# Where the rows of the second half are staged before they are normalised, and one persistent buffer for raw weights

## The chip, the cores and the metric

One Trainium2 chip, of which the kernel uses one core. The metric is device time in microseconds for one call. The engines are TensorE (PE; its weight loads are shown as PEld), VectorE (DVE), ScalarE (ACT), GpSimd (POOL) and SyncE (SP), which here only issues transfers. Each takes its own instructions strictly in order; semaphores tie them together.

## What is computed

One layer of a hybrid decoder trunk for 2048 new prompt positions and 64 sample tokens, width 1024. Every row of x is RMS-normalised and multiplied by one input projection with 33 column groups of 128; 16 of them belong to a short convolution, 17 to an RWKV-7 recurrence of 8 heads.

```python
xn = rms_norm(x, norm_g)
p = xn @ w_in
pc, pr = p[..., :CONV_COLS], p[..., CONV_COLS:]
u = cg * h
z = conv_w[0]*u_ext[:, 0:T] + conv_w[1]*u_ext[:, 1:T+1] + conv_w[2]*u_ext[:, 2:T+2]
y_conv = bg * z * silu(gc)
# recurrence, per head and token:
S = S * w_t + sa * (kk_t * a_t) + v_t * k_t ;  o_t = S r_t
y = concat([y_conv, y_rwkv]) @ w_out
return x + y, ...            # then a final rms_norm
```

## The kernel before

The prompt is worked in two halves of 1024 positions. A half has three blocks of columns (positions): block 0 with 256 positions (in the first half also with the sample tokens), blocks 1 and 2 with 384 each. `xprep(hf)` prepares a half: for each block it loads the rows (128 positions x 1024) into staging buffers, takes the sum of squares of each on ACT (L247), computes the reciprocal root on DVE (`rsqrt`, a chain of small operations), scales each row and multiplies it by the norm's weights `grow`, which lie in la0 (L263 on DVE; the third row of blocks 1 and 2 by an ACT scaling and a POOL multiplication, L260 and L261), transposes the row on PE into two PSUM banks `ax` (L282) and splits each result into a rounded high part `xh` (ACT) and the remainder `xl` (DVE, L207). So a block of 128 positions costs eight transposes, two ACT copies and two DVE subtractions. The banks `ax` are two.

`project` multiplies: for each column group and block 24 matmuls into one of two PSUM banks `pj` (xh and xl against wh, and xh against wl, over 8 row groups), then an evaluation `evac` frees the bank. In the first half `load_w` loads the raw weights of a column group in two halves into `wr`, splits them into wh and wl (ACT and POOL) and also writes these to memory (`wsp`); in the second half it loads wh and wl from there, by transfers that POOL issues, and `wr` isn't used.

There are eight steps s, four head pairs in each half: `rwkv_pair` (projections of the pair), `inverse` (a small triangular inverse: on DVE a long substitution of operations sub and xi, whose result goes to memory and back, dx, and is combined by small products `cx` on PE), `wkv` (the recurrence, a chain between PE and DVE), and `conv_group`. At step 3 the order is `rwkv_pair`, `conv_group`, `xprep(1)`, `inverse`, `wkv`, so the second half's rows are prepared while conv group 3 and the inverse of pair 3 run.

The buffers in question: tag hp, four buffers of 128x1108, hold a pair's k and rr, a conv group's u and z, and staged rows. la0 and la1 hold the low-rank inputs of a half (la), which are free between the halves; la0 then takes `grow`. `wr` is a tag with two half tiles of 128x512; the output tiles (`out_tile`, the last stage) use the same tag for scratch that nobody reads. A block's xh and xl can be overwritten when the last projection of the first half, conv group 3's, is through with that block.

The code is recorded in program order; a scheduler then decides the order on each engine and of the transfers, with its own estimates of durations, and puts the semaphores. So a change of buffers changes the order.

Of the kernel before, what the change touches and what calls it, by code (L numbers as in the profile page):

```python
# [10 lines left out]
BF16 = mybir.dt.bfloat16  # L11
# [6 lines left out]
D = 1024  # L18
CW = 512
HD = 64  # L20
KT = D // 128
# [57 lines left out]
def half_blocks(hf):  # L79
    if hf == 0:  # L80
        return [Blk(0, 330, 74, 256, 0, True, SAMP), Blk(1, 384, 0, 384, 256, False, SAMP),
                Blk(2, 384, 0, 384, 640, False, SAMP)]
    return [Blk(0, 256, 0, 256, 0, False, 0), Blk(1, 384, 0, 384, 256, False, 0),
            Blk(2, 384, 0, 384, 640, False, 0)]
# [3 lines left out]
def trunk_kernel(ctx, tc, I, O):  # L88
# [8 lines left out]
    cnt = [0]  # L97

    def T(pool, shape, tag, bufs=1, dt=F32):
        cnt[0] += 1  # L100
        return pools[pool].tile(shape, dt, tag=tag, bufs=bufs, name=f"{tag}_{cnt[0]}")
# [42 lines left out]
    def rowtile():  # L144
        return T("half", [128, HALF + SAMP], "la0", 1)[:, :D]
# [5 lines left out]
    def load_params():  # L151
        act.dma_start(out=cst[:, 128:], in_=I["consts"][:, 128:])
        act.dma_start(out=prm, in_=I["params"])
        act.dma_start(out=stc, in_=I["state_conv"])
# [50 lines left out]
    def split(hi, lo, src, eng=dve):  # L205
        copy(hi, src)
        eng.tensor_tensor(out=lo, in0=src, in1=hi.bitcast(F32), op=ALU.subtract)  # L207

    def xprep(hf):
        grow = rowtile()  # L210
        if hf == 1:
            act.dma_start(out=grow, in_=I["norm_g"].partition_broadcast(128).rearrange("p a d -> p (a d)"))
        if hf == 0:
            act.dma_start(out=cst[:, 0:128], in_=I["consts"][:, 0:128])
        xh, xl = [], []
        stage = [0]

        def staging():
            stage[0] += 1
            if stage[0] % 6 == 5:  # L220
                return T("half", [128, HALF + SAMP], "la1", 1)[:, :D]
            if stage[0] % 6 == 0 and hf == 0:
                return T("pair", [128, 32, 32], "na", 1).rearrange("p a b -> p (a b)")
            return T("half", [128, 1108], "hp", 4)[:, :D]

        for bl in half_blocks(hf):
            h = T("xn", [128, KT, bl.cols], f"xh{bl.i}", 1, F32R)
            l = T("xn", [128, KT, bl.cols], f"xl{bl.i}", 1, F32R)
            xh.append(h)
            xl.append(l)  # L230
            rows = []
            if bl.samp:
                rows.append((I["x_sample"], SAMP, bl.c0 + 128))
            for i in range(bl.np // 128):
                tok = hf * HALF + bl.p0 + i * 128
                rows.append((I["x_prompt"][tok:tok + 128, :], 128, bl.c0 + i * 128))
            ss = T("small", [128, 3], "ssx", 2)[:, :len(rows)]
            if bl.samp:
                pool.memset(ss, 1.0)
            xts = []  # L240
            for j, (src, n, o) in enumerate(rows):
                xt = staging()[:n]
                sync.dma_start(out=xt, in_=src)
                junk = l[:n, :, o:o + 128]
                if hf == 1:
                    junk = T("ch", [128, KT, 128], "c2", 4, BF16)
                act.activation(out=junk, in_=xt.rearrange("p (k c) -> p k c", k=KT), func=AF.Square,  # L247
                               accum_out=ss[:n, j:j + 1])
                xts.append(xt)
            if bl.samp:  # L250
                sync.dma_start(out=grow, in_=I["norm_g"].partition_broadcast(128).rearrange("p a d -> p (a d)"))
                sr = T("small", [128, 144], "sub", 1)[:, :KT * NB].rearrange("p (k b) -> p k b", k=KT)
                act.dma_start(out=sr, in_=I["state_shift"])
                load_params()
            dve.tensor_scalar(out=ss, in0=ss, scalar1=1.0 / D, scalar2=RMS_EPS, op0=ALU.mult, op1=ALU.add)
            r = rsqrt(ss, len(rows), 128, "n")
            for j, xt in enumerate(xts):
                n = rows[j][1]
                if bl.i and j == 2:
                    copy(xt, xt, scale=r[:n, j:j + 1])  # L260
                    pool.tensor_tensor(out=xt, in0=xt, in1=grow[:n], op=ALU.mult)  # L261
                else:
                    stt(xt, xt, r[:n, j:j + 1], grow[:n])  # L263
            if bl.samp:
                pool.memset(h[:, :, 72:74].bitcast(F32), 0.0)
                pool.memset(l[:, :, 72:74].bitcast(F32), 0.0)
                hv = h[:, :, 0:72].rearrange("p k (b j) -> p k b j", j=9)
                lv = l[:, :, 0:72].rearrange("p k (b j) -> p k b j", j=9)
                split(hv[:, :, :, 0], lv[:, :, :, 0], sr)
                xt = xts.pop(0)  # L270
                rows.pop(0)
                pool.dma_start(out=O["shift_s"], in_=xt[7:SAMP:8, :])
                ps = AX([128, KT, SAMP])
                for k in range(KT):
                    pe.transpose(out=ps[:, k, :], in_=xt[:, k * 128:(k + 1) * 128], identity=ident[:SAMP, :SAMP])
                split(hv[:, :, :, 1:9], lv[:, :, :, 1:9], ps.rearrange("p k (b j) -> p k b j", j=8))
            for xt, (_, _, o) in zip(xts, rows):
                for q in range(2):
                    ps = AX([128, 4, 128])
                    for k in range(4):  # L280
                        kk = q * 4 + k
                        pe.transpose(out=ps[:, k, :], in_=xt[:, kk * 128:(kk + 1) * 128], identity=ident)  # L282
                    split(h[:, q * 4:q * 4 + 4, o:o + 128], l[:, q * 4:q * 4 + 4, o:o + 128], ps)
            if hf == 1 and bl.i == 2:
                act.dma_start(out=O["shift_p"], in_=xts[-1][127:128, :])
        return xh, xl
# [3 lines left out]
    def load_w(src, col=None, hf=0):  # L290
        wh = T("w", [128, KT, 128], "wh", 2, F32R)
        wl = T("w", [128, KT, 128], "wl", 2, F32R)
        if hf == 1:
            pool.dma_start(out=wh, in_=wsp[col, 0])  # L294
            pool.dma_start(out=wl, in_=wsp[col, 1])
            return wh, wl
        for q in range(2):
            wr = T("w", [128, 4, 128], "wr", 2)
            sync.dma_start(out=wr, in_=src[:, q * 4:q * 4 + 4, :])
            split(wh[:, q * 4:q * 4 + 4, :], wl[:, q * 4:q * 4 + 4, :], wr, pool)  # L300
        sync.dma_start(out=wsp[col, 0], in_=wh.bitcast(F32))
        sync.dma_start(out=wsp[col, 1], in_=wl.bitcast(F32))
        return wh, wl
# [589 lines left out]
    def out_tile(woh, wol, frow, ysrc, rows, xsrc, dst):  # L893
        yr = T("half", [128, HALF + SAMP], "la1", 1)[:, :D].rearrange("p (k t) -> p k t", k=KT)[:, :, :rows]
        sync.dma_start(out=yr, in_=ysrc.rearrange("(k p) t -> p k t", p=128))
        yh = T("w", [128, KT, 128], "wh", 2, F32R)[:, :, :rows]
        yl = T("w", [128, KT, 128], "wl", 2, F32R)[:, :, :rows]
        copy(yh, yr, scale=0.5)
        stt(yl, yr, 0.5, yh.bitcast(F32), ALU.mult, ALU.subtract)
        xt = T("half", [128, 1108], "hp", 4)[:, :D][:rows]  # L900
        sync.dma_start(out=xt, in_=xsrc)
        ss = T("small", [128, 2], "ss2", 2)[:rows]
        junk = T("w", [128, D], "wr", 2, BF16)[:rows]
        for q in range(2):
            ps = PS([128, 512], "pj", 2)[:rows]
            cs = slice(q * 512, (q + 1) * 512)
            for k in range(KT):
                mm(ps, yh[:, k, :], woh[k][:, cs], start=(k == 0), stop=False)
                mm(ps, yh[:, k, :], wol[k][:, cs], start=False, stop=False)
                mm(ps, yl[:, k, :], woh[k][:, cs], start=False, stop=(k == KT - 1))  # L910
            tt(xt[:, cs], ps, xt[:, cs], ALU.add)
            act.activation(out=junk[:, cs], in_=xt[:, cs], func=AF.Square, accum_out=ss[:, q:q + 1])
        s = T("small", [128, 1], "ss", 2)[:rows]
        tt(s, ss[:, 0:1], ss[:, 1:2], ALU.add)
        dve.tensor_scalar(out=s, in0=s, scalar1=1.0 / D, scalar2=RMS_EPS, op0=ALU.mult, op1=ALU.add)
        r = rsqrt(s, 1, rows)
        stt(xt, xt, r, frow[:rows])
        act.dma_start(out=dst, in_=xt)
# [7 lines left out]
    for s in range(8):  # L926
        hf, p = divmod(s, NPAIR)
# [95 lines left out]
```

## Time and profile before

| | us |
|---|---|
| three runs | 1623.73, 1629.85, 1634.08 (median 1629.85) |
| profiled execution, device time | 1627.34 |
| its span | 1625.4 |
| PE busy, PEld busy | 1517.5 (93%), 1267.9 (78%) |
| DVE, ACT, POOL busy | 1011.9 (62%), 616.3 (38%), 290.4 (18%) |
| mean granted clock of PE | 0.966 of 2.4 GHz |

Busy time counts from the start to the end of an instruction, pipelined neighbours together; where an engine waits, the trace names what ended the wait. A granted clock of 0.50 is 1.2 GHz, of 1.00 2.4 GHz. Issue of a transfer and its landing are apart by microseconds; the trace gives both.

### The profile page before, as it was taken

What the parts mean: (1) busy time and instruction counts of PE and PEld (TensorE: products, weight loads), DVE (VectorE), ACT (ScalarE), POOL (GpSimd) and SP (SyncE); (2) the same over time, 40 slices, a digit from 0 to 9 for tenths busy, and PEclk for the clock granted to TensorE, in tenths of its full rate; (3) what the DMA queues carried; (4) which work ended last, traced back from release to release, by engine and by line L of the source; (5) the groups of instructions that cost most, each with busy time, mean ns of one, the idle gap of its engine ahead of it and who ended that gap; (6) DMA issues with size and microseconds to landing.
All of it is one profiled execution on the core that took longest, in us unless ns stands there. A gap on an engine that the chain in (4) does not pass through costs nothing.

```text
span 1625.4 us, 29341 instructions
## 1 busy us (share of the span) xinstructions
PE 1517.5 (93%) x11088; PEld 1267.9 (78%) x11088; DVE 1011.9 (62%) x3101; ACT 616.3 (38%) x1591; POOL 290.4 (18%) x395
## 2 busy tenths in 40 slices
PE   4999999989999999879999899999998999899997
PEld 4988877877788778867789678977896788667885
DVE  7387458655687458775587258635863587466544
ACT  6452345324532354344451245134413533342221
POOL 3133103311133112320022002200220022000000
PEclk9999999899999998989999899999999999899999
DMA  7323412242043213341123212321241135414441
GB/s 239 117 83 126 122 44 96 84 121 81 19 131 112 94 49 113 124 137 60 36 62 109 67 35 63 108 68 36 61 124 53 36 100 158 144 61 136 141 138 52
DMA packets 121967, 151.90 MB, mean 93 GB/s; under 512 B 62617, under 2 KB 86681, under 8 KB 121826
## 3 DMA queue, kind: packets, MB, share of 16 engines
q1 hardware_dynamic: 107024, 104.53, 20.9%
q0 software_dynamic: 9536, 34.64, 6.7%
q10 hardware_dynamic: 5266, 10.86, 1.8%
q8 instruction: 88, 1.44, 0.4%
q14 instruction: 53, 0.43, 0.1%
HBM read 92.60 MB, written 57.35 MB: 92 GB/s over the span
## 4 chain that ended last, share of the span: by engine, by line
PE 63%; DVE 22%; DMA 6%; issue 5%; ACT 3%; SPq 1%; POOL 1%; ACTq 0%; DVEq 0%; POOLq 0%
PE pj L129 41%; PE ca L129 5%; PE ax L129 5%; DVE sub L123 5%; DVE xi L123 4%; PE cb L129 4%; PE oo L129 2%; DVE hp L123 2%; PE cx L129 2%; PE cx L699 1%; DMA hp<-in_x_prompt 1%; DMA dx<-xi 1%; DVE hp L120 1%; DMA AB<-dx 1%; DMA na<-dn 1%
## 5 line engine op out<-in xcount | busy, mean ns | idle before, releaser
L129 PE MATMUL pj<-xh,wh 128*128 128x384 f32 (+3 forms) x1856 | 654.8, 353 | 17.4 <-DVE hp L123 13.7
L129 PE MATMUL pj<-xl,wh 128*128 128x384 f32 (+3 forms) x1856 | 652.6, 352 | 2.6 <-POOL xl L207 1.9
L129 PE MATMUL pj<-xh,wl 128*128 128x384 f32 (+3 forms) x1856 | 652.0, 351 | 0.6 <-DMA wl<-wsp 0.6
L129 PEld LDWEIGHTS pj<-xh,wh 128*128 128x128 f32 x1856 | 356.3, 192 | 50.1 <-DVE hp L123 11.2
L129 PEld LDWEIGHTS pj<-xl,wh 128*128 128x128 f32 x1856 | 356.8, 192 | 31.4 <-POOL xl L207 2.8
L129 PEld LDWEIGHTS pj<-xh,wl 128*128 128x128 f32 x1856 | 355.4, 191 | 28.1 <-issue 2.0
L117 ACT ACTIVATE tS<-sv,wc 64x64 f32<-64x64 f32 x256 | 88.0, 344 | 118.7 <-DVE sv L120 95.6
L207 POOL TENSOR_TENSOR wl<-wr,wh 128x512 fp32r<-128x512 f32 x66 | 87.6, 1338 | 195.1 <-ACT wh L117 191.7
L120 DVE SCALAR_TENSOR_TENSOR sv<-cb,wc,tS 64x64 f32<-64x64 f32 x240 | 68.0, 283 | 62.7 <-PE cb L129 55.0
L129 PE MATMUL ax<-L,bk 64*128 64x128 f32 x528 | 79.4, 299 | 21.0 <-DVE bk L123 12.7
L129 PEld LDWEIGHTS ax<-L,bk 64*128 64x128 f32 x528 | 66.3, 198 | 38.0 <-issue 23.2
L123 DVE TENSOR_TENSOR sub<-xi,na 128x126 f32<-128x126 f32 (+22 forms) x248 | 79.8, 322 | 16.3 <-DMA na<-dn 9.2
L117 ACT ACTIVATE t<-pj,prm 128x384 f32<-128x384 f32 (+3 forms) x170 | 68.9, 433 | 53.5 <-PE pj L129 52.4
L747 DVE TENSOR_SCALAR u<-ca,Q 128x64 f32<-128x64 f32 x128 | 36.2, 283 | 81.2 <-PE ca L129 81.0
L527 POOL TENSOR_TENSOR bk<-t,t 64x384 f32<-64x384 f32 (+2 forms) x56 | 58.0, 1036 | 144.4 <-ACT t L499 78.3
L123 DVE TENSOR_TENSOR xi<-xi,sub 128x126 f32<-128x126 f32 (+22 forms) x248 | 76.8, 310 | 7.3
L117 ACT ACTIVATE wh<-wr 128x512 fp32r<-128x512 f32 x66 | 40.5, 625 | 94.6 <-PE pj L129 74.5
L129 PEld LDWEIGHTS ca<-sv,L 128*64 128x64 f32 x528 | 43.7, 134 | 38.1 <-DVE sv L120 13.8
L737 DVE COPY xs<-ca 128x64 f32<-128x64 f32 x128 | 28.7, 224 | 66.2 <-PE ca L129 57.0
L129 PE MATMUL ca<-sv,L 128*64 128x64 f32 x528 | 68.7, 245 | 0.1
L294 POOL DMA_DIRECT2D wh<-wsp x33 | 18.7, 567 | 273.9 <-PE pj L129 199.6
L123 DVE TENSOR_TENSOR hp<-pj,hp 128x512 f32<-128x512 f32 (+1 forms) x34 | 23.4, 689 | 62.7 <-PE pj L129 62.3
(203 smaller groups left out, 2064.7 us busy)
## 6 DMA issues: line engine op xcount, KB each, us to landing
wr<-in_w_in SPq DMA_DIRECT2D x66, 256.0 KB, 3.7
wsp<-wh SPq DMA_DIRECT2D x33, 512.0 KB, 2.9
wsp<-wl SPq DMA_DIRECT2D x33, 512.0 KB, 3.9
wh<-wsp POOLq DMA_DIRECT2D x33, 512.0 KB, 3.6
wl<-wsp POOLq DMA_DIRECT2D x33, 512.0 KB, 4.5
hp<-in_x_prompt SPq DMA_DIRECT2D x29, 512.0 KB, 4.0
la<-yd SPq DMA_DIRECT2D x16, 512.0 KB, 4.0
out_y_p<-hp ACTq DMA_DIRECT2D x16, 512.0 KB, 2.6
```

The source lines that it names most:

```text
L117: act.activation(out=out, in_=in_, func=AF.Copy, scale=scale, bias=bias)
L120: eng.scalar_tensor_tensor(out=out, in0=in0, scalar=scalar, in1=in1, op0=op0, op1=op1)
L123: dve.tensor_tensor(out=out, in0=in0, in1=in1, op=op)
L129: pe.matmul(out, lhsT=lhsT, rhs=rhs, start=start, stop=stop)
L207: eng.tensor_tensor(out=lo, in0=src, in1=hi.bitcast(F32), op=ALU.subtract)
L294: pool.dma_start(out=wh, in_=wsp[col, 0])
L527: pool.tensor_tensor(out=S.bk[bl.i][hs, chs, h, :], in0=ta[hs, a:a + n].rearrange("p (c j) -> p c j", j=64), in1=wi[hs, a:a + n].rearrange ...
L699: pe.transpose(out=pb[:, i, :], in_=S.bk[bi][:, ca + i].rearrange("p a t -> p (a t)"), identity=ident)
L737: dve.tensor_copy(out=xs_, in_=px)
L747: dve.tensor_scalar(out=u, in0=pu, scalar1=S.Q[:, q:q + 1], scalar2=None, op0=ALU.mult)
```

## The change

The two half tiles of `wr` become one tile `WR` of 128x1024 that lives from the beginning; `load_w` and `out_tile` use its two halves in turn. `staging`, which gives each row its buffer, is changed for the second half: rows 1 and 2 (block 0) are in hp as before, row 3 is now in la1 (before: hp), row 4 in hp, row 5 in WR (before: la1), rows 6 to 8 (block 2) in hp. The first half's rows stay where they were.

```diff
+    WR = T("w", [128, KT, 128], "wr", 1)
+
     def xprep(hf):
@@
         def staging():
             stage[0] += 1
-            if stage[0] % 6 == 5:
+            if stage[0] == (5, 3)[hf] or stage[0] == 11:
                 return T("half", [128, HALF + SAMP], "la1", 1)[:, :D]
-            if stage[0] % 6 == 0 and hf == 0:
+            if stage[0] == 5:
+                return WR.rearrange("p k c -> p (k c)")
+            if stage[0] == 6 and hf == 0:
                 return T("pair", [128, 32, 32], "na", 1).rearrange("p a b -> p (a b)")
             return T("half", [128, 1108], "hp", 4)[:, :D]
@@
         for q in range(2):
-            wr = T("w", [128, 4, 128], "wr", 2)
+            wr = WR[:, q * 4:q * 4 + 4, :]
@@
         ss = T("small", [128, 2], "ss2", 2)[:rows]
-        junk = T("w", [128, D], "wr", 2, BF16)[:rows]
+        cnt[0] += 1
+        j = cnt[0] % 2
+        junk = WR[:rows, 4 * j:4 * j + 4, :].bitcast(BF16).rearrange("p k c -> p (k c)")
```

Where the order changes: SP's transfers at the change of halves, before. Rows of x are the ones from in_x_prompt (hp_7509 and hp_7513 are the first two of block 1, whose third, in la1, stands further up; 7584, 7588 and 7592 are block 2); dx carries the inverse's substitution to memory, AB brings it back, yd writes conv's z.

```order
L243 DMA hp_7509<-in_x_prompt 128x1024
L380 DMA yd_84<-hp_7039 128x320
L380 DMA yd_85<-hp_7039 128x384
L665 DMA dx_7788<-xi_7658 1024x1x32 x2
L243 DMA hp_7513<-in_x_prompt 128x1024
L380 DMA yd_86<-hp_7039 128x384
L243 DMA hp_7584<-in_x_prompt 128x1024
L674 DMA AB_1114_6377<-dx_7788 32x4x32
L243 DMA hp_7588<-in_x_prompt 128x1024
```

The same place in the changed kernel; hp_7448 and wr_113 are block 1's second and third row (its first, in la1, stands further up, where la1 was loaded before), hp_7518, 7522 and 7526 are block 2.

```order
L247 DMA hp_7448<-in_x_prompt 128x1024
L247 DMA wr_113<-in_x_prompt 128x1024
L384 DMA yd_84<-hp_6982 128x320
L384 DMA yd_85<-hp_6982 128x384
L439 DMA t_8461<-in_w_da 128x256
L247 DMA hp_7518<-in_x_prompt 128x1024
L384 DMA yd_86<-hp_6982 128x384
L247 DMA hp_7522<-in_x_prompt 128x1024
L247 DMA hp_7526<-in_x_prompt 128x1024
L669 DMA dx_7722<-xi_7592 1024x1x32 x2
```

The last of block 1's rows has moved up behind the one before it, and the three rows of block 2 now stand ahead of dx.

On ACT after conv group 3's last tanh (t<-pj), before: xh_1257 is block 0, xh_1270 block 1; c,ssx<-hp or la is the sum of squares of a row, hp_7513 and la_1277 of block 1, 7584 and 7588 of block 2.

```order
L376 ACTIVATE t_7444<-pj_7419 128x384
L117 ACTIVATE xh_1257_7451<-ax_7478 128x4x128
L117 ACTIVATE xh_1257_7451<-ax_7485 128x4x128
L117 ACTIVATE xh_1257_7451<-ax_7492 128x4x128
L117 ACTIVATE xh_1257_7451<-ax_7499 128x4x128
L247 ACTIVATE c_1276_7515,ssx_7508<-hp_7513 128x1024
L247 ACTIVATE c_1278_7519,ssx_7508<-la_1277_7517 128x1024
L247 ACTIVATE c_1291_7586,ssx_7583<-hp_7584 128x1024
L117 ACTIVATE la_1277_7517<-la_1277_7517,nwyn_7522 128x1024
L247 ACTIVATE c_1293_7590,ssx_7583<-hp_7588 128x1024
L117 ACTIVATE xh_1270_7506<-ax_7539 128x4x128
L117 ACTIVATE xh_1270_7506<-ax_7546 128x4x128
```

And now, where xh_1192 is block 0 and xh_1205 block 1:

```order
L117 ACTIVATE xh_1192_7386<-ax_7427 128x4x128
L117 ACTIVATE xh_1192_7386<-ax_7434 128x4x128
L251 ACTIVATE c_1225_7520,ssx_7517<-hp_7518 128x1024
L117 ACTIVATE xh_1205_7441<-ax_7473 128x4x128
L117 ACTIVATE xh_1205_7441<-ax_7480 128x4x128
L251 ACTIVATE c_1227_7524,ssx_7517<-hp_7522 128x1024
L117 ACTIVATE xh_1205_7441<-ax_7487 128x4x128
L117 ACTIVATE xh_1205_7441<-ax_7494 128x4x128
L251 ACTIVATE c_1229_7528,ssx_7517<-hp_7526 128x1024
L117 ACTIVATE xh_1205_7441<-ax_7501 128x4x128
```

Block 1's squares and the third row's scaling are gone from here (they stand ahead of the last two tanh), and block 2's three squares stand between block 1's copies.

On DVE in the middle of the inverse's substitution (sub and xi), before:

```order
L123 TENSOR_TENSOR sub_7743<-xi_7658,na_7657 128x135
L123 TENSOR_TENSOR xi_7658<-xi_7658,sub_7743 128x9x15
L123 TENSOR_TENSOR sub_7746<-xi_7658,na_7657 128x126
L123 TENSOR_TENSOR xi_7658<-xi_7658,sub_7746 128x9x14
L123 TENSOR_TENSOR sub_7749<-xi_7658,na_7657 128x130
```

The same place now; nwan and nwyn are the reciprocal root of block 1's statistics, t_7323 and hp_6982 conv group 3's gate.

```order
L123 TENSOR_TENSOR sub_7677<-xi_7592,na_7591 128x135
L120 SCALAR_TENSOR_TENSOR nwan_7457<-nwan_7457,ssx_7443 128x3
L123 TENSOR_TENSOR xi_7592<-xi_7592,sub_7677 128x9x15
L120 SCALAR_TENSOR_TENSOR nwyn_7456<-nwan_7457,nwyn_7456 128x3
L123 TENSOR_TENSOR sub_7680<-xi_7592,na_7591 128x126
L120 SCALAR_TENSOR_TENSOR la_1208_7444<-la_1208_7444,nwyn_7456,la_1191_7384 128x1024
L120 SCALAR_TENSOR_TENSOR hp_7448<-hp_7448,nwyn_7456,la_1191_7384 128x1024
L120 SCALAR_TENSOR_TENSOR t_7323<-t_7323,pj_7298 128x384
L123 TENSOR_TENSOR xi_7592<-xi_7592,sub_7680 128x9x14
```

Block 1's statistics and its two DVE scalings have moved into the substitution. On POOL the third row's multiplication (L261, now L265) has moved with them, ahead of the loads of the second half's first weights. On PE block 1's transposes now stand between block 0's matmuls, and the inverse's cx products between those of block 1; before, the first cx stood ahead of all of block 1's matmuls.

## Rows read from the trace of the kernel before

**Rows 1.** The page, part 1: busy time, share of the span, instructions.
```profile
PE 1517.5 (93%) x11088; PEld 1267.9 (78%) x11088; DVE 1011.9 (62%) x3101; ACT 616.3 (38%) x1591; POOL 290.4 (18%) x395
```

**Rows 2.** Waits of PE, 676 to 745 us: us in total, times, longest.
```profile
PE ax L282 <- DVE hp L120: 5.2, 1, 5.2
...
PE ax L282 <- DVE xl L207: 2.4, 3, 1.3
PE cx L129 <- DVE na L683: 2.4, 1, 2.4
```

**Rows 3.** Busy time by stage, with PE's granted clock behind POOL, DMA share, GB/s.
```profile
676.00:680.00 4.00, 1.46 (x10) 1.17 (x8) 4.00 (x17) 0.65 (x2) 0.99 (x1) 1.00 0.69 239
...
701.70:708.00 6.30, 6.16 (x50) 5.76 (x48) 1.19 (x2) 1.48 (x2) 0.77 (x3) 1.00 1.05 272
708.00:724.20 16.20, 6.68 (x104) 5.37 (x104) 12.54 (x38) 11.71 (x29) 4.07 (x2) 0.77 0.43 113
724.20:730.40 6.20, 6.19 (x42) 5.59 (x43) 5.91 (x7) 2.62 (x5) 3.87 (x3) 0.50 0.01 3
```

**Rows 4.** Timeline of SP's issues: start us, us, line, transfer.
```profile
675.39 0.37 SPq L243 DMA_DIRECT2D hp<-in_x_prompt  x1
...
699.10 1.29 SPq L665 DMA_DIRECT2D dx<-xi  x2
700.48 2.92 SPq L243 DMA_DIRECT2D hp<-in_x_prompt  x1
703.49 0.38 SPq L380 DMA_DIRECT2D yd<-hp  x1
...
707.62 0.33 SPq L243 DMA_DIRECT2D hp<-in_x_prompt  x1
```

**Rows 5.** Timeline of ACT: start us, us, instruction, idle time before it.
```profile
707.12 1.06 ACT L247 ACTIVATE c<-hp 128x1024 bf16<-128x1024 f32 x1 [4.58 <-DMA hp<-in_x_prompt]
```

**Rows 6.** Timeline of DVE.
```profile
672.41 1.27 DVE L123 TENSOR_TENSOR nwan<-nwyn 128x2 f32<-128x2 f32 x1
...
698.88 0.19 DVE L123 TENSOR_TENSOR xi<-xi,sub 128x16 f32<-128x16 f32 x1
...
699.44 0.68 DVE L207 TENSOR_TENSOR xl<-ax,xh 128x512 fp32r<-128x512 f32 x1
...
709.34 0.17 DVE L255 TENSOR_SCALAR ssx<-ssx 128x3 f32<-128x3 f32 x1 [6.08 <-ACT c L247]
...
711.71 2.48 DVE L120 SCALAR_TENSOR_TENSOR hp<-hp,nwyn,la 128x1024 f32<-128x1024 f32 x2
714.11 0.31 DVE L676 STREAM_TRANSPOSE na<-AB 128x128 f32<-128x128 f32 x1
```

**Rows 7.** Timeline of PE.
```profile
697.81 1.03 PE L282 MATMUL ax<-cst,hp 128*128 128x128 f32 x8
...
715.02 0.64 PE L129 MATMUL cx<-na,AB 32*32 32x32 f32 x16
...
722.29 0.57 PE L129 MATMUL cx<-AB,na 32*32 32x32 f32 x24 [2.37 <-DVE na L683]
724.21 0.69 PE L129 MATMUL pj<-xh,wh 128*128 128x384 f32 x1 [1.36 <-DVE t L120]
```

**Rows 8.** Timeline of POOL.
```profile
672.37 2.55 POOL L207 TENSOR_TENSOR wl<-wr,wh 128x512 fp32r<-128x512 f32 x2 [2.47 <-ACT wh L117]
...
693.94 0.60 POOL L294 DMA_DIRECT2D wh<-wsp  x1 [16.96 <-PE pj L129]
...
713.07 3.34 POOL L261 TENSOR_TENSOR la<-la,la 128x1024 f32<-128x1024 f32 x1 [7.01 <-ACT la L117]
...
726.30 2.46 POOL L261 TENSOR_TENSOR hp<-hp,la 128x1024 f32<-128x1024 f32 x1 [3.65 <-ACT hp L117]
```

**Rows 9.** Transfers 690 to 725 us: KB each, median us to landing.
```profile
hp<-in_x_prompt SPq DMA_DIRECT2D x4, 512.0 KB, 4.5
```

## The prediction

> **What bounds the kernel now.** I read the page's busy shares first: TensorE (PE) is busy 93% of the span [rows 1], so a change outside its matrix work pays only where PE waits. The order listings say where to look: apart from one stretch the instructions of all five engines stand in the same order with the same waits. That stretch is the change of halves, from the last blocks of the fourth conv group to the recurrence of pair 3 and the first projections of the second half, some 200 us from 686 us on. The list of PE's waits for 676 to 745 us names the largest: 5.2 us for the scaling of a row (hp, L120), then 2.4 us each for xl and for the copies between the inverse's small products [rows 2]. The table by stage shows what follows: from 708 to 724.2 us PE is busy 6.68 of 16.20 us at a mean clock of 0.77, and from 724.2 to 730.4 it is busy throughout at 0.50, which is 1.2 GHz; that second stretch alone costs half of 6.19, 3.1 us [rows 3].
>
> The cause of the 5.2 us is in SyncE's queue. Block 1's first row is loaded at 675.39. Its second row needs a buffer that block 0's transposes release, is issued at 700.48 and lands 6.6 us later: its sum of squares starts at 707.12, after 4.58 us in which ScalarE had nothing else to do [rows 4, 5]. VectorE (DVE) gets the statistics at 709.34, scales two rows from 711.71 in 2.48 us [rows 6], and only then can PE transpose. Its first matmul of block 1 starts at 724.21; block 0's, of which 48 run in 6.16 us, start at about 701.7 [rows 3, 7].
>
> **What the change does.** Block 1's rows now go to la1, to the buffer that conv's u leaves, and to WR. Listings show the WR transfer directly behind the 675.39 one, so by about 682 us all three are in. Statistics, scaling and transposes of block 1 then need not wait for block 0. That removes the 5.2 us wait as it stands. Outside this stretch I cost the new tile at nothing: the half-tile loads of WR keep their places and waits, and the output tiles' scratch halves alternate as before, so no cover is needed there.
>
> What it adds is an order in which DVE has more to do earlier. From 676 to 680 us DVE is busy 4.00 of 4.00 us [rows 3], and it stays near that with the inverse's substitution until 699.44, when it takes the first xl of block 0 [rows 6]. I go by milestones.
>
> *a. Block 0's first matmul.* Ahead of that xl DVE now also scales two rows (2.48 us), while about three substitution operations of some 0.19 us move behind it (-0.6) [rows 6]. The twelve small operations of the reciprocal root stand between dependent substitution steps and fit their latency; I take 0.2 us, at most 12 x 0.2 = 2.4. The third row's multiplication runs on GpSimd (POOL, L261), formerly at 713.07 and now in the middle of the substitution. Beside two POOL operations, together 2.55 us, a DVE operation on 128x2 took 1.27 us, where its like takes 0.17 [rows 6, 8]. But at 713.07 it was POOL that took 3.34 us instead of the 2.46 of 726.30, while DVE's scalings kept their 2.48 [rows 6, 8]. So which one waits depends on order. POOL becomes ready when ScalarE has scaled the row, by my estimate 0.1 us before DVE's first scaling ends; DVE then waits the whole 2.46. The sum is 2.48 + 2.46 + 0.2 - 0.6 = 4.5 us: block 0 starts at 706.2. If POOL lost, it would be 2.1, and the forecast below 2.4 us lower; ends 1.9 and 7.6 (3.34 and 2.4 for the open terms). Behind that multiplication POOL now queues the loads of the second half's first weights, issued at 693.94 before [rows 8]; it runs from about 691.6 to 694.1, so they are hardly later, and if it ran after both scalings they would be 2.5 us later, still landed 8 us ahead of 706. On ScalarE the third row's scaling waits for the root ahead of the tanh of the last two conv blocks; they lose about 1.5 us, hidden because DVE takes their results only behind its two scalings.
>
> The Trainium skill ("SBUF — State Buffer", section "Who interferes with whom") has a rule for this: DVE with two SBUF inputs and a reading POOL operation share one port pair, exclusively, and whichever issues first holds it for a whole instruction. By that rule either end is possible, 1626.5 or 1624.1, and the trace agrees with both of its sides (1.27 us for DVE, 3.34 us for POOL).
>
> *b. Block 0 to block 1.* 48 matmuls (6.16) and block 1's transposes, three rows of eight at 1.03 us (3.1) [rows 3, 7], now follow as one stretch. Two waits are in it. On ScalarE the squares of block 2's rows now stand ahead of block 1's xh copies, so they pace them: the first of these rows can be issued at about 701.2 (PE waits for DVE before the last conv block and ends it at about 700.1 instead of 697.8, then transposes 1.03 [rows 7]), lands 6.6 us later as at 700.48, and after square (1.06 [rows 5]), xh and xl PE gets its buffer near 710.2, where it wants it at 709.4. With the second row 1.0 us in all; ends 0 and 3. The last row waits for conv's z to be written out: write at about 704.9, 4.1 us to release (703.49 to 707.62 [rows 4]), 4.5 us to land [rows 9], 1.06 for the square, then on DVE, in order, the statistics and the last two xl of block 1 (2 x 0.68 [rows 6] and seven small operations of 0.2): 717.4. PE is through with block 0 at 706.2 + 6.2 + 3.1 + 1.0 = 716.5, so it waits 1.1; ends 0 and 3. Block 1 starts at 717.6 instead of 724.21, 6.6 us sooner.
>
> *c. What is then still due.* Before, PE had by 724.21 also done four groups of the inverse's products, from 0.64 to 0.57 us, 2.2 together [rows 7]. They now come later: -2.2. The slow stretch of 724.2 to 730.4 is no longer where it was: +3.1 [rows 3]. New: block 2's transposes wait for a scaling that DVE reaches at about 720 (0.5), and the first inverse product waits for the transpose of AB that stands behind both scalings, or not, by POOL's second multiplication (0 to 2.46, take 1.2): -1.7, ends 0 and 5.7 (rival 2).
>
> *d. The clock.* PE now waits 3.3 us once, after block 0's first transposes, and about 0.4 to 1.1 us four times. At 676 to 680 it idled 2.54 of 4.00 us and kept 1.00; over 708 to 724.2 it idled 9.5 of 16.20 and fell [rows 3]. 3.3 us lies between, nearer the first, but with more idle time around it. I charge four fifths of the measured stretch, 2.5; ends 0 and two such stretches, 6.2. The Trainium skill ("TensorE: Matmul & The Clock Gate", Part 1) says that an idle array is halved in clock and gets it back by being busy; by that rule the fall is the likelier side, and the trace agrees with its 0.50 after the wait.
>
> **Sum.** 6.6 - 2.2 + 3.1 - 1.7 - 2.5 = 3.3, with unrounded terms 3.4 us. Against the profiled execution, 1627.34 us of which 1625.4 are its span, that is 1624.0. It lay 2.5 us under the median of the three runs, so against that I take 1629.85 - 3.4 = 1626.5.
>
> **Rivals.**
> 1. *The wait goes and nothing takes its place.* DVE loses no time to POOL (a: 1.9 to 2.1), block 2's rows land as fast as the median 4.5 us [rows 9], the clock stays up. Of 14.2 us (22.55 between the two first matmuls, less 6.16, 3.1 and 2.2, plus 3.1) only 2 to 5 are lost: 1618 to 1621. For it speaks that block 1's rows are in early for certain; against it that DVE is full where the new work lands.
> 2. *The inverse becomes the wait: slower.* On SyncE the two dx writes, at 699.10 before, now stand behind the last row's load, which waits for z's write: 709.4 at the earliest. From dx to the first transpose of AB it took 15.0 us (699.10 to 714.11 [rows 4, 6]); that gives 724.4. PE reaches the first inverse product at about 722.3, and being in order it then holds the projections too. If the transfers take 3.6 us more, the wait is 5.7 us instead of 1.7, and the recurrence behind it starts later with fewer projections left beside it: 1631 to 1635. It decides once that transpose starts after about 725.5. Against it: part of the 15.0 us was DVE's own delay.
> 3. *The change does nothing that shows*: the row wait is exchanged for the 4.5 us of step a and the two waits of step b, and the clock falls as before: 14.2 - 4.5 - 2.1 - 1.7 - 6.2 = -0.3, so 1629 to 1631.
>
> **Numbers.** Forecast (1623 to 1629) 0.45, rival 1 0.23, rival 2 0.19, rival 3 0.13. The range of 8 in 10 leaves out half of the far ends: all best terms give 1629.85 - 12.3 = 1617.5, all worst 1641, which do not meet; the three runs themselves spread from 1623.73 to 1634.08. I take 1617 to 1635; the forecast's own is 1623 to 1629. Over 1% (about what a measurement of this kernel can tell from no change) means below 1613.6 or above 1646.1: the first needs more than the whole 14.2 us, the second more than the worst sum, so 0.04 and 0.02, with 0.94 within.
>
> **What would show it.** The 5.2 us wait for hp (L120) gone; the WR square done by 684 us; POOL's multiplication near 691 us and a scaling or substitution step beside it that is some 2.3 us too long; first xl of block 0 near 703.7, block 0's first matmul near 706.2, block 1's near 717.6; dx issued near 709.4. Wrong would be the forecast if block 0 starts by 704 with the clock at 1.00 throughout (rival 1), or if PE's largest wait is on the inverse's products (rival 2), or if the times before 686 us move.

## The result and the profile after

The changed kernel took 1618.17 us (median of 22 runs, 1602.56 to 1624.65) and the kernel before, on the same chip, 1626.51 us (median of 22, 1612.72 to 1636.12). The ratio is 0.9943, 95% interval 0.9925 to 0.9961: 9.3 us faster, 6 to 12. All ratios come from executions in the faster state alone and need not equal the quotient of two medians. A second comparison, below, gave 0.9967, interval 0.9936 to 0.9999. So the sign was right, the time lies within 1% of before and inside the range of 1617 to 1635, though below the forecast's own 1623 to 1629. The gain of 3.4 us was forecast too small: it lies outside the first interval and inside the second.

The page's first part, answering to [rows 1] (busy us, share of the span, instructions):

```profile
PE 1512.1 (94%) x11088; PEld 1265.4 (79%) x11088; DVE 1011.3 (63%) x3101; ACT 616.2 (38%) x1591; POOL 289.6 (18%) x395
```

This execution took 1613.0 us, with a span of 1610.9 at a mean clock of 0.969. The times of day in two traces can't be set side by side as they are: at the last point ahead of the changed stretch on DVE (the first of two subtractions of 128x120 in the inverse's substitution) before stands at 685.87 and after at 681.08, though PE, DVE and POOL have the same order up to it. (ACT and SP have not: `WR`'s load and two squares of block 1's rows already stand ahead of it.) That is scatter between executions; three traces of the changed kernel itself have the point at 671.65, 681.08 and 689.16. From here on this point is called A, and times "behind A" are counted from it.

The waits of PE from 676 to 745 us after (us in total, times, longest), answering to [rows 2]:

```profile
PE ax L286 <- DVE xl L207: 4.0, 2, 3.6
PE pj L129 <- DVE t L120: 2.1, 2, 1.4
```

The wait of 5.2 us for a scaled row is gone, and so is the 2.4 for the inverse's copies. In their place stands one of 3.6 us for the first xl. The table by stage (length, busy us of PE, PEld, DVE, ACT and POOL with counts, granted clock, DMA share, GB/s), to be held against [rows 3]:

```profile
697.80:701.70 3.90, 1.98 (x9) 1.60 (x9) 3.34 (x11) 0.60 (x1) 0.15 (x1) 0.62 0.99 358
701.70:708.00 6.30, 6.30 (x40) 6.09 (x40) 2.91 (x6) 4.53 (x9) 0.00 (x0) 0.69 0.79 210
708.00:724.20 16.20, 15.10 (x131) 13.76 (x130) 13.32 (x33) 10.52 (x24) 4.59 (x6) 1.00 0.17 35
724.20:730.40 6.20, 6.20 (x118) 5.03 (x116) 3.62 (x8) 3.23 (x8) 0.00 (x0) 1.00 0.01 3
```

From 708 to 724.2 PE is now busy 15.10 of 16.20 us, where it was 6.68 (by A the second trace is 4.8 us further on in the program at the same time of day). The clock falls earlier: the means of 0.62 and 0.69 are one stretch at 0.50, from 698.7 to 705.6, and it is back at 1.00 from then on; the stretch of 6.20 us at 0.50 is not there.

SP's issues (start, us, transfer), answering to [rows 4]:

```profile
670.59 0.37 SPq L247 DMA_DIRECT2D hp<-in_x_prompt  x1
671.00 0.78 SPq L247 DMA_DIRECT2D wr<-in_x_prompt  x1
...
696.15 0.33 SPq L247 DMA_DIRECT2D hp<-in_x_prompt  x1
700.16 0.33 SPq L384 DMA_DIRECT2D yd<-hp  x1
701.94 0.98 SPq L247 DMA_DIRECT2D hp<-in_x_prompt  x2
703.01 1.29 SPq L669 DMA_DIRECT2D dx<-xi  x2
```

ACT's square and scaling of block 1's third row and its square of block 2's last row, then POOL's two multiplications, which answer to [rows 5, 8]:

```profile
678.64 1.05 ACT L251 ACTIVATE c<-wr 128x1024 bf16<-128x1024 f32 x1
...
685.59 1.16 ACT L117 ACTIVATE wr<-wr,nwyn 128x1024 f32<-128x1024 f32 x1 [5.81 <-DVE nwyn L120]
...
708.31 1.05 ACT L251 ACTIVATE c<-hp 128x1024 bf16<-128x1024 f32 x1
```

```profile
686.83 2.39 POOL L265 TENSOR_TENSOR wr<-wr,la 128x1024 f32<-128x1024 f32 x1 [14.64 <-ACT wr L117]
...
715.66 3.40 POOL L265 TENSOR_TENSOR hp<-hp,la 128x1024 f32<-128x1024 f32 x1 [5.78 <-issue]
```

DVE, answering to [rows 6]:

```profile
685.64 1.28 DVE L120 SCALAR_TENSOR_TENSOR la<-la,nwyn,la 128x1024 f32<-128x1024 f32 x1
686.84 3.46 DVE L120 SCALAR_TENSOR_TENSOR hp<-hp,nwyn,la 128x1024 f32<-128x1024 f32 x1
...
698.99 0.68 DVE L207 TENSOR_TENSOR xl<-ax,xh 128x512 fp32r<-128x512 f32 x1
...
714.32 2.48 DVE L120 SCALAR_TENSOR_TENSOR hp<-hp,nwyn,la 128x1024 f32<-128x1024 f32 x2
716.72 0.30 DVE L680 STREAM_TRANSPOSE na<-AB 128x128 f32<-128x128 f32 x1
```

And PE, answering to [rows 7]: the first transposes of block 0, block 0's second transposes and first matmuls, block 1's first matmul, the inverse's first product:

```profile
695.09 1.04 PE L286 MATMUL ax<-cst,hp 128*128 128x128 f32 x8
699.73 2.18 PE L286 MATMUL ax<-cst,hp 128*128 128x128 f32 x8 [3.60 <-DVE xl L207]
701.56 0.78 PE L129 MATMUL pj<-xh,wh 128*128 128x256 f32 x2
...
712.81 0.45 PE L129 MATMUL pj<-xh,wh 128*128 128x384 f32 x1 [0.66 <-DVE t L120]
...
717.27 0.44 PE L129 MATMUL cx<-na,AB 32*32 32x32 f32 x16
```

The same milestones behind A, for all traces of this study (the experiments are described below). "Pair 4" is the first matmul of block 1 in the next run of projections in which all orders agree again; behind it PE's order is the same for all. The last column is the mean granted clock in the three stretches 120 to 135, 135 to 150 and 150 to 165 us behind A; the clock itself has two levels, 0.50 and 1.00, and a mean between them is a stretch of which a part ran at 0.50.

| trace | first xl | block 0 | block 1 | pair 4 | block 1 to pair 4 | clock |
|---|---|---|---|---|---|---|
| before | 13.57 | 15.79 | 38.34 | 197.40 | 159.06 | 1.00 1.00 1.00 |
| before, again (e7) | 13.59 | 15.80 | 38.33 | 196.62 | 158.29 | 1.00 1.00 1.00 |
| e1, tile only | 13.59 | 15.80 | 38.67 | 196.89 | 158.22 | 1.00 1.00 1.00 |
| after | 17.91 | 20.48 | 31.73 | 190.35 | 158.62 | 1.00 1.00 1.00 |
| after, again (e6) | 17.42 | 19.92 | 31.89 | 190.17 | 158.28 | 1.00 1.00 1.00 |
| after, third (e11) | 17.92 | 20.49 | 30.80 | 189.20 | 158.40 | 1.00 1.00 1.00 |
| e2, la1 first | 13.57 | 15.78 | 35.97 | 194.17 | 158.20 | 1.00 1.00 1.00 |
| e3, other rooms | 17.88 | 20.11 | 32.17 | 194.47 | 162.30 | 0.89 0.94 0.83 |
| e3, again (e9) | 17.89 | 20.11 | 32.31 | 193.36 | 161.05 | 1.00 0.92 0.86 |
| e4, no POOL in block 1 | 16.12 | 18.65 | 29.22 | 193.03 | 163.81 | 1.00 0.83 0.83 |
| e4, again (e8) | 16.09 | 18.62 | 29.21 | 193.09 | 163.88 | 1.00 0.83 0.83 |
| e10, no POOL in 1 and 2 | 16.11 | 18.64 | 30.06 | 191.05 | 160.99 | 1.00 0.83 0.94 |

From the middle one of the first three (196.89) to the middle one of the three of after (190.17) the changed stretch became 6.7 us shorter. That is where the time went: 6.4 to 7.9 us at block 1's start (least and most over the six traces), and next to nothing behind it.

### The profile page after: what moved, and what is told of

It is laid out like the page before. It is cut to its first block, busy times and chain, and to the rows that moved or that the text cites. A ratio compares the mean times of both kernels' runs of the same rounds, so it can differ in the third digit from the quotient of the medians.

```text
span 1610.9 us, 29335 instructions
## 1 busy us (share of the span) xinstructions
PE 1512.1 (94%) x11088; PEld 1265.4 (79%) x11088; DVE 1011.3 (63%) x3101; ACT 616.2 (38%) x1591; POOL 289.6 (18%) x395
## 4 chain that ended last, share of the span: by engine, by line
PE 63%; DVE 23%; issue 5%; DMA 5%; ACT 2%; POOL 1%; SPq 1%; ACTq 0%; DVEq 0%; POOLq 0%
PE pj L129 41%; PE ca L129 5%; PE ax L129 5%; DVE sub L123 5%; PE cb L129 4%; DVE xi L123 4%; DVE hp L123 2%; PE oo L129 2%; PE cx L129 2%; DVE hp L120 1%; PE cx L703 1%; DVE bk L123 1%; DVE t L120 1%; DMA dx<-xi 1%; DMA AB<-dx 1%
## 5 line engine op out<-in xcount | busy, mean ns | idle before, releaser
L120 DVE SCALAR_TENSOR_TENSOR sv<-cb,wc,tS 64x64 f32<-64x64 f32 x240 | 68.0, 283 | 62.6 <-PE cb L129 56.1
```

Source lines behind the costliest of these rows:

```text
L120: eng.scalar_tensor_tensor(out=out, in0=in0, scalar=scalar, in1=in1, op0=op0, op1=op1)
```

## The experiments

All kernels of the first group ran on one chip with five rounds against the kernel before, which took 1625.61 us there (median of 35).

**e1: the tile alone.** `WR` is persistent and in two parts as in the change, but every row is staged where it was.

```diff
-            if stage[0] == (5, 3)[hf] or stage[0] == 11:
+            if stage[0] == 5:
                 return T("half", [128, HALF + SAMP], "la1", 1)[:, :D]
-            if stage[0] == 5:
-                return WR.rearrange("p k c -> p (k c)")
```

> WR is one persistent tile, used by load_w and out_tile as in the changed kernel, but every row is staged where it was before. All engines have the order of the kernel before. Theory (the gain is the early rows alone): ratio to before 1.000, within 0.3%, and the 5.2 us wait of PE for hp (L120) and the slow clock after it are there. Rival (the tile itself gains, by other waits on the half tiles or on the scratch of the output tiles): ratio near 0.994 with the 5.2 us wait still there.

Measured: 1625.76 us, ratio 0.9976, interval 0.9942 to 1.0011. All five engines have the order of before, the milestones are those of before, and so is the row wait:

```profile
PE ax L284 <- DVE hp L120: 4.9, 1, 4.9
```

The tile as such costs and brings nothing in the stage. By the time alone a gain of up to 0.6% isn't excluded, but e2 and e4, which have the tile too, are at 0.9992 and 0.9993. So the gain belongs to the staging.

**e2: la1 for block 1's first row, no row in WR.** The third row of block 1 goes to hp and waits for a free buffer as before.

```diff
-            if stage[0] == (5, 3)[hf] or stage[0] == 11:
+            if stage[0] == (5, 3)[hf]:
                 return T("half", [128, HALF + SAMP], "la1", 1)[:, :D]
-            if stage[0] == 5:
-                return WR.rearrange("p k c -> p (k c)")
```

> As the changed kernel, but the fifth row of the second half (block 1's third) goes to a buffer of tag hp instead of WR; la1 takes block 1's first row. So two of block 1's three rows are early and the third waits for block 0's transposes. Theory (block 1's statistics need all three rows, the last one decides): block 1's first matmul comes about as late after the substitution's 128x120 step as before, 38 us, and the ratio to before is 1.000, within 0.3%. Rival (what gains is the new order of rows, or la1's row out of the way): 32 to 35 us and a ratio of 0.994 to 0.997.

Measured: 1623.98 us, ratio 0.9992, interval 0.9968 to 1.0017. The wait is nearly whole:

```profile
PE ax L284 <- DVE la L120: 4.1, 1, 4.1
```

The statistics of a block need all its rows. With one row late, the two early ones bring 2.4 us at block 1's start (35.97 against 38.34, where the theory had 38 and the rival 32 to 35) and 2.7 at pair 4, and nothing that the times can tell from no change.

**e3: all three rows early, the rooms in another order.** Row 3 stays in hp, row 4 goes to WR, row 5 to la1.

```diff
-            if stage[0] == (5, 3)[hf] or stage[0] == 11:
-                return T("half", [128, HALF + SAMP], "la1", 1)[:, :D]
             if stage[0] == 5:
+                return T("half", [128, HALF + SAMP], "la1", 1)[:, :D]
+            if stage[0] == 4 and hf == 1:
                 return WR.rearrange("p k c -> p (k c)")
```

> All three rows of block 1 early in the other order: first in hp, second in WR, third in la1, where it was before. Theory (only that the last of the three is early counts): block 1's first matmul 31 to 33 us after the substitution's 128x120 step, as in the changed kernel (31.7), ratio to before 0.994, within 0.3%. Rival (la1 as the first row matters): between, 34 to 36 us and 0.997.

Measured: 1622.28 us, ratio 0.9983, interval 0.9954 to 1.0012. The stage behaves as in the changed kernel: block 1 starts at 32.17, and DVE's second scaling is held while POOL multiplies. First DVE, then POOL:

```profile
698.29 1.28 DVE L120 SCALAR_TENSOR_TENSOR hp<-hp,nwyn,la 128x1024 f32<-128x1024 f32 x1
699.49 3.41 DVE L120 SCALAR_TENSOR_TENSOR wr<-wr,nwyn,la 128x1024 f32<-128x1024 f32 x1
```

```profile
699.44 2.37 POOL L265 TENSOR_TENSOR la<-la,la 128x1024 f32<-128x1024 f32 x1 [15.82 <-ACT la L117]
```

So it is having all three rows early that removes the wait, and not which row lies where. But the expected 0.994 lies outside the interval, and 3.7 of the 6.2 us won at block 1 are missing at pair 4 (194.47); where they go is taken up with e4.

**e4: the changed kernel with block 1's third row scaled on DVE**, in one instruction, without ACT's scaling and POOL's multiplication.

```diff
-                if bl.i and j == 2:
+                if bl.i and j == 2 and not (hf == 1 and bl.i == 1):
```

> As the changed kernel, but block 1's third row in the second half is scaled on DVE in one operation instead of ACT and POOL. Theory (the POOL multiplication blocks DVE for about its whole length): the second scaling falls from 3.46 to 1.24 us, the third adds 1.24, so the first xl of block 0 comes 1.0 us sooner after the substitution's 128x120 step (17.9 us in the changed kernel) and block 0's first matmul with it; ratio to the kernel before 0.9935, no difference from the changed kernel that the times can show. Rival (POOL does not hold DVE; 3.46 us has another cause): the first xl comes 1.2 us later.

Measured: 1625.92 us, ratio 0.9993, interval 0.9963 to 1.0024. With POOL away, no scaling is held:

```profile
696.43 1.28 DVE L120 SCALAR_TENSOR_TENSOR la<-la,nwyn,la 128x1024 f32<-128x1024 f32 x1
697.63 1.28 DVE L120 SCALAR_TENSOR_TENSOR hp<-hp,nwyn,la 128x1024 f32<-128x1024 f32 x1
699.29 1.28 DVE L120 SCALAR_TENSOR_TENSOR wr<-wr,nwyn,la 128x1024 f32<-128x1024 f32 x1
```

The first xl comes 1.8 us earlier than after, and block 1 2.5 us earlier. The hold of step a is thus shown: 2.2 us in one instruction (3.46 against 1.28), of which one more scaling, 1.28, would have to be taken off in exchange. Yet pair 4 starts 2.7 us later than after. Between block 1 and pair 4, e4 needs 163.81 us where after needs 158.62. The table of three stretches there, 120 to 165 us behind A, first after, then e4:

```profile
801.08:816.08 15.00, 13.65 (x90) 11.74 (x90) 12.61 (x47) 7.87 (x23) 2.86 (x5) 1.00 0.02 4
816.08:831.08 15.00, 13.61 (x88) 12.11 (x87) 13.79 (x27) 6.07 (x13) 4.62 (x9) 1.00 0.51 156
831.08:846.08 15.00, 14.41 (x87) 12.72 (x86) 12.19 (x25) 6.14 (x13) 4.50 (x8) 1.00 0.16 43
```

```profile
811.87:826.87 15.00, 13.69 (x89) 12.35 (x89) 12.31 (x48) 7.60 (x21) 3.35 (x6) 1.00 0.11 32
826.87:841.87 15.00, 13.24 (x75) 11.63 (x74) 12.43 (x24) 5.04 (x11) 3.88 (x6) 0.83 0.39 127
841.87:856.87 15.00, 14.17 (x73) 13.04 (x73) 10.29 (x19) 6.33 (x13) 4.11 (x6) 0.83 0.13 36
```

PE is idle about as long in all three (1.4, 1.4 and 0.6 us after; 1.3, 1.8 and 0.8 in e4), but in e4 the clock falls. Finer slices of e4 show that the two means of 0.83 are one stretch of some 10 us at 0.50 that lies across the border of the two:

```profile
834.37:836.87 2.50, 1.73 (x13) 1.64 (x14) 2.39 (x6) 0.00 (x0) 0.00 (x0) 0.95 0.65 216
836.87:839.37 2.50, 2.50 (x9) 2.06 (x10) 1.61 (x4) 0.00 (x0) 0.50 (x1) 0.50 0.00 0
839.37:841.87 2.50, 2.50 (x10) 1.84 (x10) 1.11 (x2) 0.00 (x0) 0.00 (x0) 0.50 0.00 0
841.87:844.37 2.50, 2.50 (x9) 1.97 (x8) 1.11 (x2) 0.00 (x0) 0.51 (x1) 0.50 0.00 0
844.37:846.87 2.50, 2.50 (x8) 2.20 (x8) 1.27 (x3) 0.74 (x2) 0.00 (x0) 0.50 0.25 39
```

PE is busy throughout it at half speed, which costs half of 10.2, 5.1 us: the 5.2 that are missing. PE's waits in the 70 us from 120 behind A, after, then e4:

```profile
PE ax L129 <- DVE bk L123: 1.3, 2, 1.0
PE ax L129 <- DVE nwag L120: 1.2, 1, 1.2
```

```profile
PE ax L129 <- DVE bk L123: 2.2, 2, 1.3
PE ax L129 <- DVE nwag L123: 1.1, 1, 1.1
```

nwag is the reciprocal root of the group norm behind pair 3's recurrence, bk an input of pair 4. Before has no wait for nwag here; all kernels with block 1's three rows early have it.

**e6 and e7: the changed kernel and the kernel before once more**, unchanged, on another chip than the first group's, with five rounds each (before: 1627.0 us, median of 23).

> The changed kernel once more, on another chip, with its profile. Theory A (the gain of the recorded comparison is real: block 1's first matmul comes 6.6 us earlier and pair 4's first block about 7 us earlier, nothing is paid back): ratio 0.994 to 0.996, and after the changed stage the granted clock stays at 1.00 in the 120 to 165 us behind the alignment point. Theory B (6.6 us are won at block 1 as before, but the thinner queue in front of pair 4's products leaves short waits there, behind which the clock falls in some executions; the 0.994 was a favourable set): ratio 0.997 to 0.999, with a stretch at 0.50 to 0.60 in these 45 us. Both expect of the stage itself, from the alignment point: first xl at 17.9, block 0's first matmul at 20.5, block 1's at 31.7, no wait of over 2 us behind a row's landing.

> The kernel before, unchanged, as its own comparison: ratio 1.000 within 0.003, which bounds what the comparison itself scatters. Its stage, from the alignment point: first xl at 13.6, block 0's first matmul at 15.8, block 1's first at 38.3, one wait of about 5 us for a row's landing; theory A and theory B expect the same here.

Measured: after 1620.43 us, ratio 0.9967, interval 0.9936 to 0.9999; before against itself 0.9999, interval 0.9966 to 1.0033. The milestones of after repeat (31.89 and 190.17), with the clock at 1.00 behind 120, which is theory A's mechanism; the ratio itself lies between A's range and B's, and its interval holds both. The 6.7 us of the traces would be 0.9959 of 1627, inside both measured intervals. So 6.7 us is the figure taken here, and the 9.3 of the first comparison holds some scatter.

**e8, e9 and e11: e4, e3 and the changed kernel again, for the trace alone.** They ask whether the fall of the clock behind 120 us is chance. (The text for e9 says "first half's"; its edit is e3's, which concerns the second half's block 1.)

> The kernel with block 1's third row scaled on DVE, once more, for its trace alone. Theory S (the clock's fall behind the short waits of pair 4's first block differs from execution to execution): the same waits (about 1.1 and 1.3 us, behind DVE), but a clock of 1.00 in the 120 to 165 us behind the alignment point, or a fall in another place; pair 4's first block then at 189 to 190 from the alignment point. Theory P (the program decides it): 0.83 in the 135 to 165 us again, and pair 4's first block at 193.

> The kernel whose first half's staging alone differs in the order of its rooms (first row in the ring, then the raw-weight buffer, then the low-rank room), once more, for its trace alone. Theory S: a clock of 1.00 in the 120 to 165 us behind the alignment point or a fall in another place, pair 4's first block between 190 and 194.5. Theory P: 0.89, 0.94 and 0.83 in the three stretches again, and pair 4's first block at 194.5.

> The changed kernel a third time, for its trace alone. Theory S: the clock may fall here too in the 120 to 165 us behind the alignment point, pair 4's first block between 190 and 194. Theory P: clock 1.00 throughout these and pair 4's first block at 190.2, as in both traces so far.

Measured: e4 fell to 0.83 in the same two stretches, with pair 4 at 193.09 against 193.03. e3 fell again, to 0.92 and 0.86, though not in the first of the three stretches, with pair 4 at 193.36. The changed kernel stayed at 1.00 a third time. So mere chance, theory S, is unlikely: seven traces of three kernels keep apart. But theory P doesn't hold to the letter either, for e3's 0.89 in the first stretch didn't come again and its second fall came in both. What decides it is open. It isn't the order behind the stage: e3 and after have the same order on all five engines from 31 us behind A on, and idle times that differ by under 0.3 us in each of the three stretches, and still one loses 2.6 to 4.0 us between block 1 and pair 4 (161.05 and 162.30 against about 158.4) and the other nothing.

**e10: the changed kernel with the third rows of blocks 1 and 2 on DVE.**

```diff
-                if bl.i and j == 2:
+                if bl.i and j == 2 and hf == 0:
```

> The changed kernel with the third rows of blocks 1 and 2 of the second half scaled on DVE in one instruction, without ACT's scaling and POOL's multiplication; behind the stage its order is the changed kernel's. Theory L (the two engines hold each other up wherever POOL's multiplication lies beside DVE's scalings): every scaling near 1.28, first xl at 16.1 and block 1's first matmul at 29.2 from the alignment point, 2.5 us ahead of the changed kernel, block 2's recurrence input no later, so pair 4's first block at 187 to 188 and a ratio of 0.992 to 0.995. Rival (DVE is the limit of block 2, and one scaling more on it costs what the hold cost; or the clock falls behind pair 4's short waits again): block 1 at 29.2 too, pair 4's first block at 190 to 193, ratio 0.996 to 0.999.

Measured: 1620.84 us against 1629.64 (median of 17) on its chip, ratio 0.9951, interval 0.9921 to 0.9982. Block 2's three scalings take 3.68 us together, none is held:

```profile
727.01 3.68 DVE L120 SCALAR_TENSOR_TENSOR hp<-hp,nwyn,la 128x1024 f32<-128x1024 f32 x3
```

Block 1 starts at 30.06, up to 1.8 us ahead of after, but pair 4 at 191.05, up to 1.9 us behind it, with the clock at means of 0.83 and 0.94 in between. That is the rival's second way: the clock takes back what the missing hold gave. The ratio lies between the two forecasts and decides nothing. By it e10 and the changed kernel can't be told apart, so no version tried is shown to beat the changed kernel.

## Why the prediction was right, and where it was too small

**The cause.** Right. e1 and e2 have the wait of 4.9 and 4.1 us for the scaled row, while every kernel with all three rows early is without it. The tile shows no cost (e1).

**Step a, block 0's first matmul 4.5 us later.** Measured 4.7, 4.1 and 4.7 in the three traces of after. The choice it rested on, that POOL starts first and DVE waits, held by 0.01 us (686.83 against 686.84), and by 0.02 in the two other traces of after. That it came out was partly luck: the forecast had no way to tell so small a lead, and by its own account the other order was worth 2.4 us. e4 shows it from the other side: without POOL, block 0 is 2.9 us late and not 4.7, at the price of one more scaling on DVE. The Trainium skill ("SBUF — State Buffer", "Who interferes with whom") says that whichever of the two issues first holds the port pair for a whole instruction. The rows agree each time: POOL first by 0.01 and 0.05 us, DVE 3.46 and 3.41; DVE first (in e2 at 713.60 against 713.74), POOL 3.35 there, 3.34 before and 3.40 after, and DVE 1.28 each.

**Step b, block 0 to block 1 in 11.4 us.** Measured 11.25, and so block 1 came 6.61 us sooner where 6.6 was said. (The two other traces of after have 11.97 and 10.31.) But that sum was right by cancelling. (Its wait for z was 717.4 less 716.5, which is 0.9 and not 1.1.) Neither wait of the step came. Of the 1.0 us for the pace of block 2's squares nothing shows. z's buffer was free sooner: its write was issued at 700.16 and both rows behind it by 702.92, at most 2.8 us later and not 4.1. And ACT squares that last row at 708.31 with no idle time before it, so nothing waited for the row. The 0.66 us that PE did wait at block 1's start is for an evaluation on DVE (t, L120). A term of the sum was too large as well: four of block 1's transposes set between matmuls hold these up by 0.35 us at full clock (706.49 to 706.84), so eight cost about 0.7 and not 1.03. Against all that, 6.3 us of this stretch ran at a mean of 0.69, which costs 1.95. The clock was charged as a step of its own and summed behind block 1; in fact it fell ahead of block 1.

**Step c.** The 2.2 us of inverse products and the 3.1 us of slow clock were of the right kind. The second is uncertain by itself: behind block 1's start the clock is still at 0.50 for 6.2 us in before's first trace, but for 3.8 in e1 and e7, which is worth 3.1 and 1.9 us. The 1.7 us for waits on the inverse is the first term that failed. No wait for cx or na is in the list, and PE idles 1.2 us in all from 30 to 60 behind A, about 0.4 at those places. dx was issued at 21.9 behind A (forecast 23.5), the transpose of AB came 13.7 us behind it and not 15.0, and POOL's second multiplication lost to DVE (3.40, while the scalings kept 2.48).

**Step d, 2.5 us for the clock, is the second term that failed**, by its place. Of the three traces of after none shows a clock under 1.00 between 40 us behind A and pair 4. The fall itself came, but ahead of block 1: once at 0.50, for 6.8, 3.4 and 3.4 us in the three traces. Its price is thus inside steps a and b, and b had room for it because its two waits didn't come. With c and d, 3.8 us of the 4.2 us charged behind block 1 did not come there.

**What no step held.** The waits for nwag and bk, 120 to 180 us behind A: PE idles 2.6 us there before, 3.3 to 3.7 after. The forecast took the rest of the stretch for unchanged. In the changed kernel that cost 0.8 to 1.1 us; in e3, e4 and e10 it cost 2.7 to 5.6 with the clock (their 160.99 to 163.88 against 158.3). Nothing in the forecast could tell that the changed kernel would be spared the fall.

**Sum.** Forecast behind block 1: -2.2 + 3.1 - 1.7 - 2.5 = -3.3. Measured: block 1 to pair 4 took 159.06 before and 158.62 after, +0.4. That is the whole of what 3.4 us lacks to the 7.05 of these two traces. From block 1's start to 120 us behind A, and from there to pair 4, before, then after:

```profile
724.21:805.87 81.66, 81.49 (x702) 62.24 (x703) 46.01 (x150) 37.97 (x109) 7.56 (x11) 0.96 0.15 48
805.87:883.27 77.40, 74.61 (x493) 68.37 (x492) 57.81 (x155) 28.59 (x70) 20.28 (x30) 1.00 0.25 75
```

```profile
712.81:801.08 88.27, 87.75 (x853) 67.75 (x854) 49.37 (x167) 42.61 (x125) 7.51 (x11) 1.00 0.15 46
801.08:871.43 70.35, 66.66 (x423) 61.20 (x422) 54.86 (x146) 25.07 (x59) 20.25 (x30) 1.00 0.29 84
```

PE idles 2.96 us before and 4.21 after, 1.25 more, and saves the 3.1 of slow clock. So 3.1 - 1.25 - 0.4 leaves about 1.4 us for the work that came behind block 1, where 2.2 were charged. One of the four groups of products had been timed at half clock (0.64 where it takes 0.44), and between matmuls a group holds these up by less than its length (0.37 of the 0.44 at 717.27).

**The rivals.** 1618 to 1621, rival 1's time, is what was measured (1618.17 and 1620.43), but not by its mechanism: DVE did lose to POOL and the clock did fall. Part of it is the base: the forecast was set on a median of three runs, 1629.85, and more runs put before at 1626.5. Rival 2 (the inverse becomes the wait) is excluded by the list of waits. Rival 3 had block 1 start as the forecast had it and differed in the clock behind it; it is excluded by the clock of 1.00 from there to pair 4, and by pair 4's start. Of the conditions that would make the forecast wrong, "if the times before 686 us move" was badly chosen: they moved by 4.8 us, as they do between executions of one kernel.

## What to carry to other kernels

When an edit removes a wait, follow the freed work to the place where all orders meet again, and measure there: a start 9 us earlier (e4) can be worth 4. Charge each loss, the clock above all, at one place only and say where it falls. A block whose statistics need all its rows gains only a part from early rows (2.4 of 6.6 us here) until the last one is early too.

## What was unexpected of the hardware

The clock's fall behind waits of 1 to 1.3 us looks like more than chance, and could not be read from the amount of idle time: with 1.4, 1.4 to 1.7 and 0.6 us idle in three successive 15 us it stayed at 1.00 in the changed kernel in three traces of three, and with 1.3, 1.8 and 0.8 us it fell to 0.50 for 10 us in e4 in two of two. The Trainium skill ("TensorE: Matmul & The Clock Gate", Part 1) has the array halved in clock when idle and restored by being busy; these traces agree with the fall and show no rule for which short wait brings it.

Over a stretch whose order on PE is the same in all, the executions differ by more than the change: A lies between 671.65 and 696.31 us in the twelve traces. Two executions of the changed kernel took 1601.28 and 1620.88 us at mean clocks of 0.984 and 0.968.
